# Loads, filler products and order at the two ends of a hybrid diffusion step on one core

## The chip, the cores and the metric

The kernel runs on one core of a Trainium2 chip. The metric is the device time of one execution in microseconds (us), taken as the median over runs. The profile below is that of one further execution, and its rows count from that execution's first instruction.

## What is computed

One inference step of a small backbone with two layers, in float32: layer 0 mixes tokens with a bidirectional state-space scan (SSD), layer 1 with differential attention, and each is followed by a channel mixer (up-projection, depthwise convolution, gated product, down-projection). There are 512 latent tokens and 128 context tokens, held together as 640 columns, and 1024 features, held as 8 tiles of 128 partitions. What the change touches is the very first norm with its modulation, and the very last norm:

```
m  = silu(cvec) @ mod_w + mod_b            # six rows of 1024 a layer: shift, scale, gate, twice
h  = rmsnorm(x, g) * (1 + scale) + shift   # ahead of each sub-layer
...
xs = xs + s_g2 * conv_ffn(modulate(xs, ...))
y  = rmsnorm(xs, final_norm_g)
```

`cvec` is one vector for the context tokens and another for the latent tokens.

## The kernel before

Every matrix product is made of three passes of reduced-precision products: weights and activations are split into a high and a low part (`whi`, `wlo`, `h00h`, `h00l`), and the three larger cross products are added. `cast` makes the split of one weight tile `raw`: ScalarE (ACT) copies the high part, VectorE (DVE) subtracts it for the low part. A product on plain float32 operands shows as two matmul instructions in the trace.

All instructions go through a wrapper, so almost every row of the profile has the line L95; rows are told apart by the names of their tiles. Most of the program is ordered by a planner of the framework, which walks the instructions of each engine in the order in which they were written down and lets a `high_priority` block go first. The stretch at the start, `silu_cond` and `first_tiles`, is under `manual_schedule`: each engine runs it exactly in the order written.

The start, in that order. SyncE's queue (SP) issues all loads: `c32` (the two condition vectors repeated 16 times, 128 KB), `cst` (identity, two triangles, a column block of ones and a selector, 210 KB), the eight activation tiles `x` (320 KB each), the first two weight tiles, the biases `modb` and gains, then the modulation weights `mp` in four quarters q of eight 256 KB steps k, with another weight tile behind the first quarter. The squares `sq` of x are taken by ACT for even tiles and DVE for odd ones. `rms_rows` sums them on TensorE (PE) with `ones` as weights into `ms` and runs nine small DVE instructions (`rs_v`, `rs_a`, `rs_y`) for the reciprocal root; `rms_bcast` then spreads the row over 128 partitions with four products, `nbc`. `rows(q, k0, k1)` multiplies steps k0 to k1 of quarter q of the modulation weights by the condition (`modrow`), four groups of 32 columns at a time; `finish(q)` transposes the copied row (`modt`), adds the bias (`mod`) and makes the scale `gs`. Three steps of `rows(0, ...)` stand ahead of the broadcast and five behind it. Then `bc` is copied from `nbc` by ACT, `scaled(i)` multiplies x by it on DVE, `high(i)` makes the high part of h on ACT and the full value on DVE, `low(i)` the low part on DVE, and `dense(ws, k)` does the products of feature tile k for the first weight tiles (rows `in`). The loop over q repeats this for the feature pairs 2 to 7.

The end. `project_last` computes the last three output tiles of the down-projection in two parts of the columns: part C (columns 0 to 384), then part D (384 to 640), each tile as rows `po`. `gate_add` adds a tile's result to the residual `xr` on DVE and `norm_sq` squares it on ACT. After a part a task `final_task` is queued: it sums the squares (`ms`), does the reciprocal root, broadcasts (`nbc`), and `out_tiles` multiplies the eight residual tiles (`yt`) and issues their stores. Six of part C's tiles (`CTILES`) go out as they come; the other two are held until the end of part D's reciprocal root (`self.root`). Part D's eight follow, their stores on SP and on ACT's queue in turn.

The lines around the first broadcast are

```
st = self.rms_bcast(lambda: self.wide("nbc"), sq, 0, T, D)
next(st)
self.cast(0)
self.cast(1)
rows(0, 0, 3)
```

PSUM tiles of the start come from a pool of three (`dense_ps`): one for `nbc`, two for the first two `in` tiles, and the third `in` tile takes the place of `nbc`.

Of the kernel before, what the change touches and what calls it, by code (L numbers as in the profile page):

```python
# [11 lines left out]
F32 = mybir.dt.float32  # L12
# [33 lines left out]
DOTS = 4, 24, 28, 40, 48  # L46
CTILES = 6
TH = T // 2
# [307 lines left out]
class Step:  # L356
# [129 lines left out]
    def cast(self, upto):  # L486
        while len(self.wcast) <= min(upto, len(self.units) - 1):
# [31 lines left out]
            else:  # L519
# [6 lines left out]
                else:  # L526
                    self.act(hi[:, c], r[:, c], AF.Copy)
                    self.tt(lo[:, c], r[:, c], hi[:, c].bitcast(F32), ALU.subtract)
            self.wcast[u] = (hi, lo)
# [47 lines left out]

    def rms_bcast(self, alloc, sq, t0, t1, count, wait=4, behind=False):


        n = (t1 - t0) // 4
        y = self.rms_rows(sq, t0, n, count, behind)
        yield wait
        bc = alloc()
        for j in range(4):
            self.mm(bc[:, j * n:(j + 1) * n], self.sel[:, j:j + 1].to_broadcast([P, P]), y, True, True)
        return bc

    def rms_rows(self, sq, t0, n, count, behind=False):

        ms = self.bank("m", "ms")
        gate = self.last if behind else None
        for i, s in enumerate(sq):
            for j in range(4):
                o = self.mm(ms[32 * j:32 * j + 32, :n], self.ones, s[:, t0 + j * n:t0 + (j + 1) * n],
                            i == 0, i == len(sq) - 1)
                if behind:
                    self.hold(o, [gate])
        y = self.pc.tile([P, 160], F32, tag="rs_y", name="rs_y", bufs=1)[:, :n]
        with self.urgent(1.6) if self.later else nullcontext():  # L600
# [40 lines left out]
    def norm_stats(self, half):  # L641

        tag = {"A": "y", "B": "m", "C": "y", "D": "m"}[half]
        return self.rms_bcast(lambda: self.bank(tag, "nbc"), self.nsq, *HALF[half], D, 3, half == "B")

# [54 lines left out]
    def project_last(self, h, ks, g, nextnorm, ks_last=None, parts="AB", save=False, before=(), first=None):  # L700
# [26 lines left out]
        for hf in parts:  # L727
            for grp in ((ws[0:1], ws[1:3]) if hf == "B" else (ws[0:1], ws[1:2], ws[2:3])):
                self.dense_many([(ps, w, P) for ps, w, i in grp], ks, h, hf)
                with self.tc.high_priority() if hf == "B" else nullcontext():  # L730
                    for ps, w, i in grp:
                        self.gate_add(i, ps, g, hf)
                        self.norm_sq(i, hf)
# [83 lines left out]
    def silu_cond(self, pool):  # L817

        c32 = self.slot("f", "c32", bufs=NF)[:, :KT * 32].rearrange("p (k c) -> p k c", c=32)
        self.nc.sync.dma_start(c32, self.a["c32"])  # L820
        self.s32 = pool.tile([P, KT, 32], F32, tag="s32", name="s32", bufs=1)
        self.silu_small(self.s32, c32)

    def first_tiles(self, h, pool):
# [67 lines left out]

        self.cst = self.ct([P, 3 * P + 36], "cst")
        nc.sync.dma_start(self.cst, a["cst"])
        for i in range(KT):
            xi = self.xslot(f"x{i}")
            nc.sync.dma_start(xi, a["xT"][i])
            self.x.append(xi)
        self.prefetch(1)
        self.load_consts()  # L900
        gs, sh = self.gs[0][0], self.shift(0, 0)
        load(0)
        self.prefetch(2)
        for q in range(1, 4):
# [3 lines left out]
        for i in range(KT):  # L908
            if i % 2:
                self.tt(sq[i], self.x[i], self.x[i], ALU.mult)  # L910
            else:
                self.act(sq[i], self.x[i], AF.Square)
        st = self.rms_bcast(lambda: self.wide("nbc"), sq, 0, T, D)
        next(st)
        self.cast(0)
        self.cast(1)
        rows(0, 0, 3)
        try:
            next(st)
        except StopIteration as e:  # L920
            bps = e.value
        bc = self.slot("f", "bc", bufs=NF)
        self.act(bc, bps, AF.Copy)
        scaled(0, bps)
        scaled(1, bps)
        h.extend(self.new_h("h00"))
        rows(0, 3, KT)
        finish(0)
        ws = [(self.dense_ps("in"), self.wcast[i], P if i else 64) for i in range(2)]
        half = KT // 2  # L930
        high(0)
        low(0)
        high(1)
        low(1)
        self.cast(2)
        self.wi = 3
# [1071 lines left out]
def _layout(i):  # L2008
# [5 lines left out]
    cc = np.stack([n["c_ctx"], n["c"][0]])  # L2014
    d["c32"] = np.tile(cc.reshape(2, KT, P).transpose(2, 1, 0), (1, 1, 16))
    d["cbc"] = np.broadcast_to(cc[None], (P, 2, D))
# [61 lines left out]
```

## Time and profile before

| what | value |
|---|---|
| time, median of 3 runs | 1780.58 us (1779.38 to 1784.31) |
| time of the profiled execution | 1780.09 us |
| its span, first to last instruction | 1778.3 us |
| mean granted TensorE clock | 0.996 |
| PE busy | 1744.0 us, 98% of the span |
| DVE busy | 1471.3 us, 83% |
| ACT busy | 1170.2 us, 66% |
| DMA | 300.66 MB, mean 169 GB/s |

PE is the matmul side of TensorE and PEld its weight loads; SP and ACTq rows are DMA issues. A row of the timeline gives start, duration, engine, operation with output and inputs, count of merged instructions, and in brackets the idle time of that engine before it with what ended the idle time. Durations of merged rows run from the first start to the last end.

### The profile page before, as it was taken

What the parts mean: (1) busy time and instruction counts of PE and PEld (TensorE: products, weight loads), DVE (VectorE), ACT (ScalarE), POOL (GpSimd) and SP (SyncE); (2) the same over time, 40 slices, a digit from 0 to 9 for tenths busy, and PEclk for the clock granted to TensorE, in tenths of its full rate; (3) what the DMA queues carried; (4) which work ended last, traced back from release to release, by engine and by line L of the source; (5) the groups of instructions that cost most, each with busy time, mean ns of one, the idle gap of its engine ahead of it and who ended that gap; (6) DMA issues with size and microseconds to landing.
All of it is one profiled execution on the core that took longest, in us unless ns stands there. A gap on an engine that the chain in (4) does not pass through costs nothing.

```text
span 1778.3 us, 33599 instructions
## 1 busy us (share of the span) xinstructions
PE 1744.0 (98%) x12786; PEld 1667.6 (94%) x12786; DVE 1471.3 (83%) x2947; ACT 1170.2 (66%) x2313; POOL 150.2 (8%) x180
## 2 busy tenths in 40 slices
PE   7999999999999999999999999999999999999997
PEld 5899999989989999999999999999889999999997
DVE  5789999999967879798689799899878677867686
ACT  3479696969524767666675578777547566756661
POOL 0000000000000111211210000000001012121210
PEclk9999999999999999999999999999999999999998
DMA  9744344345663686978867365666138358686882
GB/s 346 261 145 131 115 120 150 106 145 165 223 214 130 150 205 153 253 181 216 191 167 249 114 171 132 157 153 167 56 119 207 116 144 200 175 196 156 171 234 79
DMA packets 120206, 300.66 MB, mean 169 GB/s; under 512 B 13950, under 2 KB 21738, under 8 KB 120044
## 3 DMA queue, kind: packets, MB, share of 16 engines
q1 hardware_dynamic: 94636, 231.79, 39.9%
q0 software_dynamic: 24832, 66.20, 20.8%
q8 instruction: 100, 1.64, 0.4%
q14 instruction: 62, 0.51, 0.1%
q10 hardware_dynamic: 576, 0.52, 0.1%
HBM read 248.32 MB, written 34.80 MB: 159 GB/s over the span
## 4 chain that ended last, share of the span: by engine, by line
PE 72%; DVE 5%; ACT 2%; issue 1%; DMA 1%; DVEq 0%; ACTq 0%
PE up L95 27%; PE po L95 24%; PE st L95 4%; PE z L95 2%; PE q L348 2%; PE v L348 2%; PE k L348 2%; PE sl L348 2%; PE ov L348 1%; PE po L348 1%; PE yp L95 1%; PE wt L348 1%; PE nbc L95 1%; PE modrow L95 0%; DVE sm L348 0%
## 5 line engine op out<-in xcount | busy, mean ns | idle before, releaser
L95 ACT ACTIVATE whi<-raw 128x1024 fp32r<-128x1024 f32 (+2 forms) x233 | 198.8, 855 | 163.9 <-PE po L95 77.3
L95 DVE TENSOR_TENSOR wlo<-raw,whi 128x1024 fp32r<-128x1024 f32 (+2 forms) x170 | 162.4, 961 | 54.1 <-ACT whi L95 51.7
L95 PE MATMUL po<-mh,whi 128*128 128x256 f32 (+1 forms) x704 | 165.0, 307 | 0.8 <-ACT y L95 0.5
L95 PE MATMUL po<-ml,whi 128*128 128x256 f32 (+1 forms) x704 | 164.4, 306 | 0.3 <-DMA ml<-cv 0.3
L95 PE MATMUL po<-mh,wlo 128*128 128x256 f32 (+1 forms) x704 | 164.4, 306 | 0.0
L95 DVE TENSOR_TENSOR wlo<-s,whi 128x512 fp32r<-128x512 f32 x136 | 91.2, 686 | 53.4 <-ACT whi L95 53.1
L95 POOL DMA_DIRECT2D wlo<-in_w_up x62 | 54.0, 871 | 945.0 <-ACT wlo L95 646.7
L95 PEld LDWEIGHTS po<-mh,whi 128*128 128x128 f32 x704 | 126.0, 188 | 1.9 <-ACT y L95 0.9
L95 PEld LDWEIGHTS po<-ml,whi 128*128 128x128 f32 x704 | 126.2, 188 | 0.6 <-DMA ml<-cv 0.6
L95 PEld LDWEIGHTS po<-mh,wlo 128*128 128x128 f32 x704 | 126.2, 188 | 0.0
L95 PE MATMUL up<-Th,wlo 128*128 128x320 f32 x408 | 125.7, 308 | 0.0
L95 PE MATMUL up<-Tl,whi 128*128 128x320 f32 x408 | 125.3, 307 | 0.0
L95 PE MATMUL up<-Th,whi 128*128 128x320 f32 x408 | 123.7, 303 | 0.2 <-ACT uraw L95 0.2
L95 PE MATMUL up<-h11h,wlo 128*128 128x320 f32 (+2 forms) x384 | 109.0, 307 | 0.0
L95 PE MATMUL up<-h01h,wlo 128*128 128x320 f32 (+2 forms) x384 | 109.0, 307 | 0.0
L95 PE MATMUL up<-h11l,whi 128*128 128x320 f32 (+2 forms) x384 | 108.7, 307 | 0.0
L95 PE MATMUL up<-h01l,whi 128*128 128x320 f32 (+2 forms) x384 | 108.7, 307 | 0.0
L95 PE MATMUL up<-h11h,whi 128*128 128x320 f32 (+2 forms) x384 | 107.7, 304 | 0.1
L95 PE MATMUL up<-h01h,whi 128*128 128x320 f32 (+2 forms) x384 | 107.6, 304 | 0.0
L95 ACT ACTIVATE whi<-s 128x512 fp32r<-128x512 f32 x136 | 83.3, 628 | 36.9 <-DVE s L95 33.1
L95 DVE SCALAR_TENSOR_TENSOR ca<-uraw,fcw,ca 128x511 f32<-128x511 f32 (+1 forms) x176 | 86.1, 544 | 11.3 <-ACT ca L95 9.7
L95 DVE SCALAR_TENSOR_TENSOR cv<-uraw,fcw,cv 128x511 f32<-128x511 f32 (+1 forms) x176 | 85.6, 543 | 4.9 <-ACT cv L95 4.8
(574 smaller groups left out, 5415.3 us busy)
## 6 DMA issues: line engine op xcount, KB each, us to landing
raw<-in_w_up SPq DMA_DIRECT2D x88, 512.0 KB
mw<-in_modT SPq DMA_DIRECT2D x44, 512.0 KB
raw<-in_w_in SPq DMA_DIRECT2D x40, 512.0 KB
rb<-rowd SPq DMA_DIRECT2D x40, 512.0 KB
wlo<-in_w_up POOLq DMA_DIRECT2D x36, 512.0 KB, 5.8
raw<-in_w_dn SPq DMA_DIRECT2D x64, 256.0 KB
raw<-in_w_qkv SPq DMA_DIRECT2D x24, 512.0 KB
mr<-in_mod SPq DMA_DIRECT2D x44, 256.0 KB
```

The source lines that it names most:

```text
L95: return later.record(self.name, method, call, args, kw) if later else call(*args, **kw)
L348: op.real = op.call(*(x.get() if isinstance(x, Lazy) else x for x in op.args), **op.kw)
```

## The change

At the start, the condition is loaded in two columns only (8 KB) and widened on DVE after the SiLU. The constants come in three pieces: ones and selector first, the identity behind the first two weight tiles, the triangles behind the first quarter of modulation weights. The activation tiles are issued alternately on SP's and ACT's queue, ahead of all but the first constants. DVE clears a tile; TensorE runs 12 products of 128x128 by 128x512 in bfloat16 on these zeros, then one behind the sums of each of the first seven activation tiles and five behind the eighth. Five steps of modulation instead of three stand ahead of the broadcast. Behind it come the scaling of tile 0, the other three steps, `finish(0)`, and the scaling of tile 1; the scaling no longer stands behind the copy `bc`, which moves behind `high(1)`. The second half of one weight tile's low part moves behind `low(1)`.

At the end, the gate-add and the squares of part D get priority, five instead of six of part C's tiles go out before part D's root, and ten float32 products of 128x128 by 128x128 stand between part D's sums and its broadcast.

```diff
-CTILES = 6
+CTILES = 5
...
                     self.act(hi[:, c], r[:, c], AF.Copy)
-                    self.tt(lo[:, c], r[:, c], hi[:, c].bitcast(F32), ALU.subtract)
+                    minus = lambda c: self.tt(lo[:, c], r[:, c], hi[:, c].bitcast(F32), ALU.subtract)
+                    if u == 1:
+                        minus(slice(0, n // 2))
+                        self.second = lambda: minus(slice(n // 2, n))
+                    else:
+                        minus(c)
...
-        y = self.rms_rows(sq, t0, n, count, behind)
+        y = self.rms_rows(sq, t0, n, count, behind, between)
+        if fill:
+            gate, ps = self.last, self.psb.tile([P, 512], F32, tag="b", name="warm")
+            for _ in range(fill):
+                o = self.mm(ps[:, :P], self.ident, self.U, True, True)
+                self.hold(o, [gate])
         yield wait
...
+            if between:
+                between(1 if i < len(sq) - 1 else 5)
...
-        return self.rms_bcast(lambda: self.bank(tag, "nbc"), self.nsq, *HALF[half], D, 3, half == "B")
+        return self.rms_bcast(lambda: self.bank(tag, "nbc"), self.nsq, *HALF[half], D, 3, half == "B",
+                              fill=10 if half == "D" else 0)
...
-                with self.tc.high_priority() if hf == "B" else nullcontext():
+                with self.tc.high_priority() if hf in "BD" else nullcontext():
...
     def silu_cond(self, pool):
-        c32 = self.slot("f", "c32", bufs=NF)[:, :KT * 32].rearrange("p (k c) -> p k c", c=32)
-        self.nc.sync.dma_start(c32, self.a["c32"])
+        nc = self.nc
+        self.zero = self.tmp("zero").bitcast(BF16)[:, :P + 512]
+        nc.vector.memset(self.zero, 0.0)
+        self.cst = self.ct([P, 3 * P + 36], "cst")
+        nc.sync.dma_start(self.cst[:, 3 * P:], self.a["cst"][:, 3 * P:])
+        for i in range(KT):
+            xi = self.xslot(f"x{i}")
+            (nc.scalar if i % 2 else nc.sync).dma_start(xi, self.a["xT"][i])
+            self.x.append(xi)
+            if i == 1:
+                c2, s2 = (self.ct([P, KT, 2], n) for n in ("c2", "s2"))
+                nc.sync.dma_start(c2, self.a["c2"])
         self.s32 = pool.tile([P, KT, 32], F32, tag="s32", name="s32", bufs=1)
-        self.silu_small(self.s32, c32)
+        self.act(s2, c2, AF.Tanh, scale=0.5)
+        self.stt(s2, s2, 1.0, c2, ALU.add, ALU.mult)
+        nc.vector.tensor_scalar(self.s32.rearrange("p k (r c) -> p k r c", c=2),
+                                s2.unsqueeze(2).to_broadcast([P, KT, 16, 2]), 0.5, None, ALU.mult)
...
-        self.cst = self.ct([P, 3 * P + 36], "cst")
-        nc.sync.dma_start(self.cst, a["cst"])
-        for i in range(KT):
-            xi = self.xslot(f"x{i}")
-            nc.sync.dma_start(xi, a["xT"][i])
-            self.x.append(xi)
+        wps = self.dense_ps("warm")[:, :512]
+        def warm(n):
+            for _ in range(n):
+                self.mm(wps, self.zero[:, :P], self.zero[:, P:], True, True)
+        warm(12)
         self.prefetch(1)
+        nc.sync.dma_start(self.cst[:, :P], a["cst"][:, :P])
         self.load_consts()
         gs, sh = self.gs[0][0], self.shift(0, 0)
         load(0)
+        nc.sync.dma_start(self.cst[:, P:3 * P], a["cst"][:, P:3 * P])
         self.prefetch(2)
...
-        st = self.rms_bcast(lambda: self.wide("nbc"), sq, 0, T, D)
+        st = self.rms_bcast(lambda: self.wide("nbc"), sq, 0, T, D, between=warm)
         next(st)
         self.cast(0)
         self.cast(1)
-        rows(0, 0, 3)
+        rows(0, 0, 5)
...
-        bc = self.slot("f", "bc", bufs=NF)
-        self.act(bc, bps, AF.Copy)
         scaled(0, bps)
+        rows(0, 5, KT)
+        finish(0)
         scaled(1, bps)
         h.extend(self.new_h("h00"))
-        rows(0, 3, KT)
-        finish(0)
...
         high(1)
+        bc = self.slot("f", "bc", bufs=NF)
+        self.act(bc, bps, AF.Copy)
         low(1)
+        self.second()
         self.cast(2)
```

More of the change, by code (lines that the diff above doesn't have):

```diff
@@ L576, in rsqrt, with rms_bcast @@
         self.root = self.stt(y, a, 5.0, y, ALU.add, ALU.mult)
-    def rms_bcast(self, alloc, sq, t0, t1, count, wait=4, behind=False):
+    def rms_bcast(self, alloc, sq, t0, t1, count, wait=4, behind=False, fill=0, between=None):
         n = (t1 - t0) // 4
-        y = self.rms_rows(sq, t0, n, count, behind)
+        y = self.rms_rows(sq, t0, n, count, behind, between)
[4 more added lines that the diff above has]
+                self.hold(o, [gate])
         yield wait
@@ L587, in rms_bcast, with rms_rows @@
         return bc
-    def rms_rows(self, sq, t0, n, count, behind=False):
+    def rms_rows(self, sq, t0, n, count, behind=False, between=None):
         ms = self.bank("m", "ms")
@@ L2014, in _layout @@
     cc = np.stack([n["c_ctx"], n["c"][0]])
-    d["c32"] = np.tile(cc.reshape(2, KT, P).transpose(2, 1, 0), (1, 1, 16))
+    d["c2"] = cc.reshape(2, KT, P).transpose(2, 1, 0)
     d["cbc"] = np.broadcast_to(cc[None], (P, 2, D))
```

## The prediction, made before the changed kernel ran

> **What bounds the kernel now.** I read the page first. TensorE is busy nearly all the time and off the middle of the span there is little to win without fewer products.
>
> ```profile
> PE 1744.0 (98%) x12786; PEld 1667.6 (94%) x12786; DVE 1471.3 (83%) x2947; ACT 1170.2 (66%) x2313; POOL 150.2 (8%) x180
> PEclk9999999999999999999999999999999999999998
> ```
>
> The span is 1778.3 us, so PE lacks 34 us, and the change touches only the two ends. So I read the timeline of both ends, then transfers and granted clock there. The start, from the last squares to the second set of modulation rows:
>
> ```profile
> 12.15 0.82 DVE L95 TENSOR_TENSOR sq<-x 128x640 f32<-128x640 f32 x1 [0.83 <-DMA x<-in_xT]
> 13.04 0.76 PE L95 MATMUL ms<-sq,cst 128*32 128x160 f32 x8 [0.16 <-DVE sq L95]
> 13.87 0.33 DVE L95 TENSOR_SCALAR rs_v<-ms 128x160 f32<-128x160 f32 x1 [0.89 <-PE ms L95]
> 15.10 0.20 PEld L95 LDWEIGHTS modrow<-mp,s 128*32 128x32 f32 x8 [1.86 <-DMA mp<-in_modp]
> 15.79 0.20 PEld L95 LDWEIGHTS modrow<-mp,s 128*32 128x32 f32 x8 [0.48 <-DMA mp<-in_modp]
> 16.46 0.20 PEld L95 LDWEIGHTS modrow<-mp,s 128*32 128x32 f32 x8 [0.47 <-DMA mp<-in_modp]
> 17.05 2.50 PE L95 MATMUL nbc<-rs_y,cst 128*128 128x160 f32 x8
> 19.48 1.30 PE L95 MATMUL modrow<-mp,s 128*32 128x128 f32 x40
> 19.59 0.70 ACT L95 ACTIVATE bc<-nbc 128x640 f32<-128x640 f32 x1 [4.29 <-PE nbc L95]
> 20.32 1.55 DVE L95 TENSOR_TENSOR h<-x,nbc 128x640 f32<-128x640 f32 x2 [1.60 <-ACT bc L95]
> 20.85 0.28 ACT L95 ACTIVATE modrow_s<-modrow 128x128 f32<-128x128 f32 x1 [0.56 <-PE modrow L95]
> 21.79 0.16 DVE L95 TENSOR_TENSOR mod<-modt,modb 128x8 f32<-128x8 f32 x1
> 22.18 2.29 ACT L95 ACTIVATE h00h<-h,mod,gs 128x512 fp32r<-128x512 f32 x4 [1.06 <-DVE gs L95]
> 23.42 0.82 DVE L95 TENSOR_TENSOR h00l<-h,h00h 128x640 fp32r<-128x640 f32 x1 [0.43 <-ACT h00h L95]
> 24.99 1.27 PE L95 MATMUL in<-h00l,whi 128*64 128x256 f32 x4
> 26.19 1.08 PE L95 MATMUL modrow<-mp,s 128*32 128x128 f32 x32
> 27.20 0.85 PE L95 MATMUL in<-h00h,whi 128*128 128x256 f32 x4
> 28.85 1.08 PE L95 MATMUL modrow<-mp,s 128*32 128x128 f32 x32
> 31.16 0.17 DVE L95 TENSOR_TENSOR mod<-modt,modb 128x8 f32<-128x8 f32 x1 [2.67 <-PE modt L95]
> ```
>
> The last activation tile lands at 12.15, the root is ready at about 17.0, the broadcast takes 2.5, and `bc` then holds DVE until 20.32. The weights arrive 0.68 us a step (15.10, 15.79, 16.46). From 26.19 on PE goes on without a gap, so what the products of tile 0 gain stays, as long as loads keep up. The stretches and the loads of the first 30 us:
>
> ```profile
> 21.00:22.00 1.00, 0.33 (x1) 0.14 (x1) 0.96 (x4) 0.12 (x1) 0.00 (x0) 1.00 1.03 375
> 23.00:24.00 1.00, 0.95 (x3) 0.85 (x4) 0.58 (x1) 1.00 (x3) 0.00 (x0) 0.50 1.06 393
> 30.00:34.00 4.00, 4.00 (x52) 3.59 (x53) 2.34 (x7) 2.57 (x5) 0.00 (x0) 1.00 1.05 387
> DMA  0049996997999999999999999999999999999999
> GB/s 0 0 147 264 258 259 239 358 314 277 382 399 417 406 401 424 391 350 376 382 391 385 385 382 412 385 410 380 371 391 388 396 385 388 388 385 371 388 391 380
> ```
>
> In a stretch the last three columns are granted clock, transfer share and GB/s; the clock is 0.50 in 23 to 24 and 1.00 in 30 to 34, where PE is full. Transfers are saturated from 7.5 us on at about 390 GB/s, and slower before.
>
> The end:
>
> ```profile
> 1761.25 1.08 PE L95 MATMUL nbc<-rs_y,cst 128*128 128x96 f32 x8
> 1762.37 2.71 DVE L95 SCALAR_TENSOR_TENSOR yt<-xr,gains,nbc 128x384 f32<-128x384 f32 x5 [1.23 <-PE nbc L95]
> 1764.34 0.28 PE L95 MATMUL po<-ml,whi 128*128 128x256 f32 x1
> 1764.45 0.28 PE L95 MATMUL po<-mh,wlo 128*128 128x256 f32 x1
> 1766.04 0.60 DVE L95 SCALAR_TENSOR_TENSOR xr<-po,mod,xr 128x128 f32<-128x128 f32 x2
> 1766.11 0.32 PE L95 MATMUL ms<-sq,cst 128*32 128x64 f32 x8 [1.01 <-ACT sq L95]
> 1766.68 0.42 ACT L95 ACTIVATE sq<-xr 128x256 f32<-128x256 f32 x1 [0.62 <-DVE xr L95]
> 1767.15 0.44 PE L95 MATMUL ms<-sq,cst 128*32 128x64 f32 x8 [0.72 <-ACT sq L95]
> 1767.66 0.22 DVE L95 TENSOR_SCALAR rs_v<-ms 128x64 f32<-128x64 f32 x1 [1.01 <-PE ms L95]
> 1769.96 1.14 DVE L95 SCALAR_TENSOR_TENSOR yt<-xr,gains,nbc 128x384 f32<-128x384 f32 x2
> 1770.07 1.94 PE L95 MATMUL nbc<-rs_y,cst 128*128 128x64 f32 x8 [2.48 <-DVE rs_y L95]
> 1772.05 3.22 DVE L95 SCALAR_TENSOR_TENSOR yt<-xr,gains,nbc 128x256 f32<-128x256 f32 x8 [0.95 <-PE nbc L95]
> 1767.00:1770.00 3.00, 0.44 (x8) 0.20 (x8) 2.03 (x10) 0.10 (x1) 0.00 (x0) 0.51 0.17 65
> ```
>
> The last product ends at about 1764.7, but its gate-add waits behind scaled tiles until 1766.04, and the last broadcast takes 1.94 for 64 columns at half clock, against 1.08 for 96 columns before.
>
> **Start: loads.** Ahead of the modulation weights 338 KB (c32 128, cst 210) become 90 (18 + 8 + 64), so 248 KB less, 0.65 us at 390 GB/s. Behind the first quarter the triangles give back 128 KB, so later quarters gain 0.3. The small pieces: three transfers more; their rows are at least free and at most as dear as the 128-packet transfer of 210 KB that they replace (0.5); I take free. The second queue: transfers are 9 tenths busy in the slow stretch too, so I price it at 0, up to 2.0 (rival two).
>
> So step k4 of quarter 0, before 15.10 + 4 x 0.68 = 17.8, lands at 17.2; k7, before 19.9, at 19.2. The last x lands at about 11.4 (0.65 to 0.8 earlier).
>
> **Start: zeros.** PE can start after DVE's clear, at about 1.2 us (0.1 to 0.8 for the clear, by the smallest and the 128x640 DVE rows). No 512-column bfloat16 product stands in the trace; products of 256 columns start 0.11 to 0.12 apart (1764.34, 1764.45), and 512 columns are an estimate of 0.23, or 0.47 at half clock. Twelve take 2.8 to 5.6 us and are over before the first sums (6 us). With the clock up, sums of a tile (0.76 cold, by the granted clock about 0.5 warm) and one filler are 0.7, under the 0.83 between tiles, so they cost nothing. Five behind the last take 1.2, inside the root's 3.2.
>
> **Start: broadcast.** Root: last x 11.4 + 0.82 + 0.1 + 0.5 + 3.2 gives 16.0. But now five steps stand ahead on PE, and k4 lands at 17.2; so the broadcast begins at 17.5, 0.45 later than before. On a warm clock it takes 1.3 instead of 2.5: the same eight instructions in the attention layer, at full clock, are
>
> ```profile
> 1294.25 1.29 PE L348 MATMUL obc<-rs_y,cst 128*128 128x160 f32 x8
> ```
>
> It ends at 18.8 (before 19.55). The other three steps end with k7 at 19.5 (before 20.8), since 0.26 a step hides under the 0.68 of loading. From there to `h00h` it took 1.4; 0.3 of that was DVE busy on the second scaling, which now stands behind `gs`; 1.1 remain, so `h00h` starts at 20.6, 1.6 earlier. DVE then does the second scaling (0.75), the full value (0.75) and `h00l` (0.82): `h00l` ends 2.35 after `h00h` starts, before 2.06. So it ends at 22.95 instead of 24.24, and tile 0's last four products, 0.74 warm instead of 1.27, end at 23.8 instead of 26.2. The copy `bc` (0.70) moves on ACT behind four activations (2.29) and ends about 23.6, ahead of its reader and of the third `in` tile. DVE's later pile (half a low part 0.6, a full one 1.2, two scalings 1.55) ends at 27.9, before 28.5, and DVE then stood idle 2.67 ahead of the next `mod` (31.16): no cost.
>
> Do loads follow? Quarter 1's steps: after 19.9 come 512 KB (1.3) and 0.68 a step, k3 at 23.9 and k7 at 26.6; with 0.3 less 23.6 and 26.3. The two sets of rows would start at 23.8 and 26.5 (before 26.19 and 28.85). They fit by 0.2, and each later set has more slack. **Start: 2.3 us**, with ends 0.3 (below) and 4.
>
> **End.** With priority the gate-adds of the second and third D tile go ahead of scaled tiles that are ready. The last product at 1764.7, at worst one scaled tile of 0.54 (2.71 for five) in flight, so the gate-add ends at 1765.5 instead of 1766.6; square, sums, root follow: the root 1.1 earlier, at 1768.8 (bounds 0.5 and 1.3, for none to two scaled tiles ahead). The fifth scaled tile fits into the 1.0 that DVE waits there. One more held tile costs DVE 0.54 behind the root: three end at 1770.5 instead of 1771.1. The ten products are twenty instructions; eight of 96 columns took 0.11 each, those of 160 columns 0.14, so 0.12, 2.4 us, beside a root of 2.3: at most 0.3 late. The broadcast then begins at 1769.1 and, warm, takes 0.9, over before DVE is free at 1770.5. The eight tiles, 3.22, thus begin at 1770.5 instead of 1772.05. Their stores (1 MB) keep pace as before; three C stores go out 0.6 earlier than two did. **End: 1.5 us** (bounds -0.8 and 1.8).
>
> **Sum.** 2.3 + 1.5 = 3.8 off the profiled execution's 1780.09 (span 1778.3 and 1.8 around it): 1776.3. That execution stood 0.5 under the median of the three runs, so the median to compare is 1776.8. The planner between the ends may set a few instructions otherwise; no row prices that, and the three runs' own distance (1.2 below and 3.7 above the median) bounds it.
>
> **Rivals.**
> One: the clock falls while PE waits for k0 to k4 (0.27 of work in each 0.68), so the broadcast takes 2.5. Then it ends at 20.0, three steps end at 20.75, `h00h` starts at 21.85, and tile 0 is done at 25.1: 1.1 instead of 2.3, so 1778.0. For it: at 1767 the clock fell to 0.51 although PE had idled only 1.01 and 0.72 us; at 23 it fell after 1.6 us of work in 3.4. Against: the five fillers and the broadcast close the gap from both sides. The Trainium skill ("TensorE: Matmul & The Clock Gate", Part 1: The HAM clock gate) has the clock fall after an idle window of about 3.4 us, so never here, and would give 1776.8; the trace disagrees, the clock was 0.51 with no such gap, so the rival keeps its chance.
>
> Two: the slow loads of 1.5 to 7.5 us (mean 265 GB/s) were the single queue's and the wide-row constants' doing. At 395 the missing 0.78 MB are 2.0 us, and since steps k4, k7 and quarter 1 all wait for loads, all of it counts: 1774.8. Against: the engines were mostly 9 tenths busy then. The Trainium skill ("DMA: Bandwidth & Descriptors", Issuing engines are not separate DMA queues) says that issuing from several engines saves no more than issue time, which speaks against this rival: by it 1776.8, by the slow stretch 1774.8. No run here has yet issued loads from two queues.
>
> Three: the end's filler runs at half clock. Twenty at 0.24 are 4.8 us from 1766.5, so the broadcast starts near 1770.9 and the last tiles gain nothing or lose up to 0.8: 1778.3 to 1779.1. For it: the fall at 1767 above. Against: the root comes 1.1 earlier and the fillers follow the sums at once.
>
> Four, the slower side: zeros do not raise the clock. Then a tile's sums and filler cost 0.76 + 0.47 = 1.23 on PE, over the 0.83 between loads, and PE becomes the start's bound: from 6.9 eight tiles end at 16.7, fillers at 19.0, five steps at 21.5, the broadcast at 24.0, and `h00h` starts at 25.9, 3.7 late. Less 1.5 at the end: 1782.8. It decides as soon as sums and filler exceed 0.83. Against: the broadcast itself raised the clock within one stretch.
>
> **How the numbers follow.** Main case 0.5 (1775.0 to 1778.3), rival one 0.2, two 0.15, three 0.1, four 0.05. The prediction is the main case, 1776.8. For 8 in 10 I go down past rival two by the runs' own 1.2 (1773.4) and up past rivals one and three together (1779.5) by as much (1780.8). A measurement can tell 0.3%, 5.3 us, so 1775.2 and below is faster: four fifths of rival two and three tenths of the main case, 0.27. Slower, above 1785.9, needs rival four and a reordered middle: 0.02. The rest, 0.71, is the same.
>
> **What would show it.** Start: `ms` of 160 columns at 0.5 per eight; five `modrow` sets then `nbc` at 17.5 for 1.3; `h00h` at 20.6; the second quarter's first rows at 23.8. End: gate-adds within 0.5 of the last `po`, `rs_v` at 1766.5 less the start's gain, `nbc` under 1.0, and a gap from root to the first 256-column `yt` of 1.7. Wrong would be: x landing no earlier, `nbc` at 2.5, a clock under 1.00 behind 1766, or waits for `mp` in the later quarters.

## The result, and the profile after

The changed kernel takes 1785.41 us (median of 22 runs, 1781.37 to 1788.17), the kernel before 1780.82 on the same chip (22 runs, 1778.35 to 1784.93): ratio 1.0024, 95% interval 1.0018 to 1.0030. The forecast was 1776.8 with a range up to 1780.8; the change is 0.24% slower instead of 0.2% faster. The profiled execution of the changed kernel took 1781.37 us, the lowest of its runs (span 1779.4, before 1778.3). So the traces explain about 1 us directly, and the median has to be settled by the experiments.

The timeline of the changed kernel, beginning (columns: start, length, engine, line, operation, tiles; in brackets the idle time before and what ended it):

```profile
0.74 5.26 ACTq L95 DMA_DIRECT2D x<-in_xT  x4
1.26 5.30 PE L95 MATMUL warm<-zero 128*128 128x512 bf16 x12 [1.26 <-DVE zero L95]
6.03 1.28 ACT L95 ACT_TABLE_LOAD   x1 [6.03 <-DMA x<-in_xT]
7.45 0.72 ACT L95 ACTIVATE sq<-x 128x640 f32<-128x640 f32 x1
9.71 0.93 SPq L95 DMA_DIRECT2D mp<-in_modp  x2
12.35 0.80 SPq L95 DMA_DIRECT2D mp<-in_modp  x2
12.36 0.83 DVE L95 TENSOR_TENSOR sq<-x 128x640 f32<-128x640 f32 x1 [2.08 <-DMA x<-in_xT]
13.33 0.48 PE L95 MATMUL ms<-sq,cst 128*32 128x160 f32 x8
16.99 0.43 PE L95 MATMUL modrow<-mp,s 128*32 128x128 f32 x8 [0.96 <-DMA mp<-in_modp]
18.29 0.43 PE L95 MATMUL modrow<-mp,s 128*32 128x128 f32 x8 [0.88 <-DMA mp<-in_modp]
18.65 1.35 PE L95 MATMUL nbc<-rs_y,cst 128*128 128x160 f32 x8
19.93 0.86 PE L95 MATMUL modrow<-mp,s 128*32 128x128 f32 x24
21.96 1.20 ACT L95 ACTIVATE h00h<-h,mod,gs 128x512 fp32r<-128x512 f32 x2 [0.82 <-DVE gs L95]
25.61 1.94 PE L95 MATMUL modrow<-mp,s 128*32 128x128 f32 x32
```

Read it from the bottom: tile 0 starts (`h00h`) at 21.96 because the first quarter's products end at 20.79 (before: 20.78, so up to here nothing is gained), because step k4 came only at 18.29. Between two steps lie 1.3 us there instead of 0.68. Higher up is the cause: SP issues two `mp` steps at 9.71, then nothing until 12.35. At 12.36 the square of the last x tile starts, so SP waited for that tile's landing (its third step waits for the semaphore that the last x load raises). ACT shows the same at 6.03: its table load waits for an x load, and the first square comes at 7.45.

The same stretches as sums (columns: stretch, its length, PE busy with the count of its instructions, granted clock, share of transfers, GB/s), changed kernel; before had 389 and 387 GB/s here:

```profile
7.00:13.50 6.50, 5.28 (x68) 1.00 1.02 367
13.50:19.50 6.00, 4.14 (x59) 1.00 0.92 285
```

What SP's DMA queue waited for in the first 20 us (total, times, longest), changed kernel:

```profile
SPq L95 <- DMA x<-in_xT: 4.0, 3, 2.0
```

Before, the same waits came in small pieces:

```profile
SPq L95 <- DMA x<-in_xT: 3.6, 7, 0.8
```

Clock at the start of the changed kernel, cut along its clock changes:

```profile
17.29:20.70 3.41, 2.53 (x47) 1.00 0.99 336
20.70:24.10 3.40, 1.70 (x11) 1.00 1.03 384
24.10:27.51 3.41, 3.32 (x38) 0.50 1.06 393
```

The zeros did raise the clock, and the broadcast took 1.35. But after a stretch in which PE was busy for 1.70 of 3.40 us (it waits for `h00h`) the next 3.41 us ran at half clock, just where tile 0's products and the second quarter's rows stand (1.94 for 32).

The end of the changed kernel:

```profile
1767.39 0.28 PE L95 MATMUL po<-mh,wlo 128*128 128x256 f32 x1
1767.70 0.61 DVE L95 SCALAR_TENSOR_TENSOR xr<-po,mod,xr 128x128 f32<-128x128 f32 x2
1768.82 0.32 PE L95 MATMUL ms<-sq,cst 128*32 128x64 f32 x8 [0.68 <-ACT sq L95]
1769.07 2.50 PE L95 MATMUL warm<-cst 128*128 128x128 f32 x20
1769.28 0.22 DVE L95 TENSOR_SCALAR rs_v<-ms 128x64 f32<-128x64 f32 x1
1771.58 4.80 DVE L95 SCALAR_TENSOR_TENSOR yt<-xr,gains,nbc 128x384 f32<-128x384 f32 x11
1771.69 1.07 PE L95 MATMUL nbc<-rs_y,cst 128*128 128x64 f32 x8
```

From the last `po` to the root's first instruction are 1.9 us (before 3.2), and the broadcast takes 1.07 instead of 1.94, beside scaled tiles on DVE. But all of it stands later: the last `po` came at 1764.45 before.

Where it slipped shows in one row a kernel, the feed-forward products of `Th` and `whi` (ns min/median/max, first and last start). Before:

```profile
L95 PE MATMUL up<-Th,whi x408: 302/303/418, 657.6 to 1716.3; 128*128 128x320 f32 x136
```

Changed kernel:

```profile
L95 PE MATMUL up<-Th,whi x408: 304/309/417, 657.7 to 1719.2; 128*128 128x320 f32 x136
```

The first such product is 0.1 late, the last 2.9. The products stand in two stretches, one in each layer; the time between the stretches is no longer than before (490.1 us before, 489.7 in the changed kernel). In the last 220 us PE is full in both kernels, and yet they hold fewer products in the changed one. First before, then changed:

```profile
1500.00:1720.00 220.00, 219.88 (x1526) 1.00 0.76 176
```

```profile
1500.00:1720.00 220.00, 220.00 (x1519) 1.00 0.76 174
```

Seven products of about 0.145 us are the 1 us that this stretch loses. The modelled length of one went from 303 to 309, the mean distance from its start to the next from 140 to 147 ns, and 408 x 7 ns is 2.9 us. The only thing that the change did to these products is their place in memory: `c2` and `s2`, 64 bytes a partition each, lie in the pool of constants, and everything allocated behind it on that side (weights, activations) moves by 128 bytes, while `Th`, `Tl` and the residual on the other side stay.

In the profiled execution the bill is 0.1 at 657, 2.8 more by 1716, and 1.8 back at the end (from the first product of part D, 1756.24 before and 1759.14 after, to the end of the span): 1.1, as the spans say.

### The profile page after: what moved, and what is told of

It reads as the page before. It is cut to its first block, busy times and chain, and to the rows that moved or that the text cites. A ratio compares the mean times of both kernels' runs of the same rounds, so it can differ in the third digit from the quotient of the medians.

```text
span 1779.4 us, 33690 instructions
## 1 busy us (share of the span) xinstructions
PE 1753.6 (99%) x12830; PEld 1674.1 (94%) x12830; DVE 1471.8 (83%) x2949; ACT 1170.8 (66%) x2313; POOL 150.2 (8%) x180
## 4 chain that ended last, share of the span: by engine, by line
PE 90%; DVE 5%; DMA 3%; ACT 1%; issue 1%; SPq 0%; DVEq 0%; ACTq 0%
PE up L95 28%; PE po L95 24%; PE z L95 5%; PE x L95 5%; PE st L95 5%; PE bc L95 3%; PE yp L95 3%; PE v L348 2%; PE q L348 2%; PE k L348 2%; PE sl L348 2%; PE ov L348 2%; PE po L348 1%; DMA mp<-in_modp 1%; PE wt L348 1%; DMA raw<-in_w_in 1%
## 5 line engine op out<-in xcount | busy, mean ns | idle before, releaser
L95 DVE TENSOR_TENSOR wlo<-raw,whi 128x512 fp32r<-128x512 f32 (+3 forms) x171 | 163.0, 960 | 54.0 <-ACT whi L95 53.6
```

The lines of the kernel that those rows point to most:

```text
L95: return later.record(self.name, method, call, args, kw) if later else call(*args, **kw)
```

## The experiments

All times are medians in us; "before" is the kernel before, run on the same chip beside each group. Ratios are to it, with 95% intervals; they are taken from the single runs and are not quotients of the medians (e4 stands at 1.0012 by the medians). The groups e1 to e8, e9 to e12 and e13 to e16 ran on three chips, so across groups the ratios are the ones to compare.

| kernel | time | before | ratio | span of its profile |
|---|---|---|---|---|
| e1 before, shifted 128 bytes | 1784.46 | 1780.85 | 1.0016 (1.0007 to 1.0025) | 1781.8 |
| e2 change without the shift | 1781.63 | 1780.85 | 1.0000 (0.9991 to 1.0009) | 1778.0 |
| e3 end alone | 1779.43 | 1780.85 | 0.9986 (0.9977 to 0.9995) | 1777.2 |
| e4 start alone, no shift | 1783.04 | 1780.85 | 1.0005 (0.9994 to 1.0015) | 1777.6 |
| e5 e4 on one queue | 1782.13 | 1780.49 | 1.0012 (1.0003 to 1.0020) | 1780.7 |
| e6 e2 on one queue | 1782.31 | 1780.49 | 1.0012 (1.0001 to 1.0022) | 1780.8 |
| e7 e5 without zeros | 1781.08 | 1780.49 | 1.0001 (0.9993 to 1.0010) | 1781.4 |
| e8 before, shifted 64 bytes | 1781.61 | 1780.49 | 1.0006 (0.9997 to 1.0014) | 1779.8 |
| e9 e5, small loads on POOL | 1780.55 | 1780.26 | 1.0002 (0.9994 to 1.0011) | 1786.3 |
| e10 e6, gap filled | 1781.18 | 1780.26 | 1.0002 (0.9993 to 1.0011) | 1779.7 |
| e11 e6, small loads on POOL and gap filled | 1777.76 | 1780.26 | 0.9985 (0.9977 to 0.9994) | 1775.8 |
| e12 e3, gap filled | 1777.78 | 1780.26 | 0.9986 (0.9978 to 0.9995) | 1776.8 |
| e13 e11, gap not filled | 1779.72 | 1779.63 | 1.0000 (0.9991 to 1.0009) | 1775.5 |
| e14 e11 on two queues | 1776.89 | 1779.63 | 0.9986 (0.9977 to 0.9995) | 1774.4 |
| e15 e11 with the shift | 1782.26 | 1779.63 | 1.0014 (1.0004 to 1.0023) | 1778.1 |
| e16 e11, three steps ahead | 1779.13 | 1779.63 | 0.9995 (0.9986 to 1.0004) | 1775.1 |

### The shift by itself: e1, e2, e8

e1 takes the kernel before and adds 128 unused bytes; e2 takes the change and puts the two tiles elsewhere; e8 is e1 with 64 bytes (`[P, 16]`).

```diff
 # e1
         self.cst = self.ct([P, 3 * P + 36], "cst")
+        self.pc.tile([P, 32], F32, tag="padc", name="padc", bufs=1)
 # e2
-                c2, s2 = (self.ct([P, KT, 2], n) for n in ("c2", "s2"))
+                c2, s2 = (self.slot("f", n, bufs=NF)[:, :2 * KT].rearrange("p (k c) -> p k c", c=2) for n in ("c2", "s2"))
```

> The kernel before with one unused tile of 128 bytes a partition in the pool of constants, which moves every left-hand buffer behind it by 128 bytes, as the two small condition tiles of the change do, and nothing else. Theory A (address shift: products whose weights are in shifted buffers and whose activations are not, up<-Th,whi, take 147 ns apart instead of 140): the feed-forward stretches run some 1.3 us longer each, the D part of the end starts 2.5 to 3 us later, and the time is 1783.4 (+2.6). Theory B (the middle drifts by another cause, such as the order of instructions or chance between executions): no change, 1780.8, and up<-Th,whi stays at 140 ns.

> The changed kernel with its two small condition tiles in the rotating buffers instead of the pool of constants, so that the later buffers keep the addresses of before modulo 512 bytes. Theory A: the drift of 2.6 us in the middle goes, the time falls to about 1782.8 (from 1785.4), and 2 us above before remain for the start. Theory B: it stays at 1785.4.

> The kernel before with an unused 64 bytes a partition in the constants pool instead of 128: weights and activations of the left-hand pools move by 64 bytes, the sums Th and Tl stay. In before, the weights whi stand 128 bytes from Th modulo 256; a shift of 128 gave both the same place modulo 256. If the cost is that coincidence, a shift of 64 leaves the products of Th and whi at 140 ns and the time within 1 of before. If any distance but before's costs, the spacing is about 147 ns and the time 3 above, as with 128. Moving operands that no longer start on a multiple of 64 bytes don't arise, since 64 is kept.

The same row of e1, of e2 and of e8:

```profile
L95 PE MATMUL up<-Th,whi x408: 304/309/418, 657.0 to 1719.8; 128*128 128x320 f32 x136
```

```profile
L95 PE MATMUL up<-Th,whi x408: 302/303/415, 658.9 to 1717.9; 128*128 128x320 f32 x136
```

```profile
L95 PE MATMUL up<-Th,whi x408: 304/307/417, 657.9 to 1718.0; 128*128 128x320 f32 x136
```

Against before (657.6 and 1716.3) e1 goes from 0.6 early to 3.5 late with not one instruction changed, e2 from 1.3 late to 1.6 late, e8 from 0.3 to 1.7. So a shift of 128 bytes costs 3 to 4 us over the two stretches, 2.9 of them in these 408 products, and taking it away gives that back. The second stretch alone, in which PE is full, parts all the profiles: from its first to its last such product it takes 283.5 or 283.6 us in the fourteen kernels without a shift, 285.0 to 285.2 in the three with 128 bytes (changed kernel, e1, e15), and 284.5 in e8. By time it is +3.6 in e1 and -3.8 from the changed kernel to e2 (medians; the changed kernel ran in another group). With 64 bytes the products stand between (307; 145 ns from start to start), the drift is 1.4, and the time, +1.1, isn't told from none. The guess of a coincidence modulo 256 bytes alone falls, and so does the guess that any other distance costs the same. Distance between the two operands isn't the whole of it either: the products of `h01h` and `whi`, both of which move by the same 128 bytes, also grow, from a mean of 303 to 305. What about the addresses counts stays open.

### The two ends apart: e3, e4

e3 is the kernel before with the changed end (`CTILES = 5`, the ten products, priority for D); e4 is e2 with the end of before.

> The kernel before with the changes of the end alone (priority of part D, five tiles out first, ten products as filler). Theory A: from the first product of part D to the end 20.3 us instead of 22.1, as in the profile of the change, and the time 1779.0 (-1.8). Rival: the filler is caught at half clock in most executions, since the window of the clock is free-running, and the gain is 0 to 0.5: 1780.5.

> The changed kernel with the end of before, and with the two small tiles in the rotating buffers (no shift). Theory A (the start is not faster, since later loads became slower and the last activation tile waits): the start is 0 to 2 us later than before, 1781 to 1783. Rival (the start gains in most executions, and the profile was an exception): 1779 or less.

The end is worth 0.14% by the ratio (2.5 us), 1.4 us by the medians and 1.7 in the profile (20.4 us from the first product of part D to the end, before 22.1); its root and broadcast have the lengths of the changed kernel's. The timeline of e3:

```profile
1769.22 4.80 DVE L95 SCALAR_TENSOR_TENSOR yt<-xr,gains,nbc 128x384 f32<-128x384 f32 x11
1769.33 1.07 PE L95 MATMUL nbc<-rs_y,cst 128*128 128x64 f32 x8
```

The start alone gains nothing: 2.2 above before by the medians, ratio 1.0005. Its trace repeats the gap in the loads (the stretch 13.5 to 19.5 of e4):

```profile
13.50:19.50 6.00, 4.14 (x58) 1.00 0.95 302
```

Medians add up: 3.6 (shift) - 1.4 (end) + 2.2 (start) = 4.4, against 4.6 measured. The ratios are less kind: 0.16 - 0.14 + 0.05 = 0.07%, each with some 0.09 either way, so about 0.16 for the sum, against 0.24 (0.18 to 0.30). They meet only at the edge.

### What the loads wait for: e5, e6, e9

e5 is e4 with all x tiles on SP, e6 the same with the changed end, e9 is e5 with the four small loads on POOL.

```diff
 # e5, e6
-            (nc.scalar if i % 2 else nc.sync).dma_start(xi, self.a["xT"][i])
+            nc.sync.dma_start(xi, self.a["xT"][i])
 # e9: c2, cst[:, :P], modb and gains
-        nc.sync.dma_start(self.cst[:, :P], a["cst"][:, :P])
+        nc.gpsimd.dma_start(self.cst[:, :P], a["cst"][:, :P])
...
```

> The new start without the shift of addresses and with the end of before, and all eight x tiles loaded by SP instead of alternately by SP and ACT. Theory (loads take eight completion semaphores in turn, so the second queue only makes ACT and then SP wait in order for an older load): ACT's table load and first square come some 1.5 to 2 us earlier, SP issues the steps of the modulation without a gap of 2 us, the transfer rate in 13 to 19 us is back near 390 GB/s, steps k3 and k4 land 0.7 apart, and the broadcast of 160 columns begins by 17.6 and takes 1.3; time 1.0 to 2.0 below the kernel with two queues and 0.5 to 2 below before. Rival (the rate falls because of the additional small pieces, whatever the queue): the rate stays near 300 GB/s in 13 to 19 us, k4 lands at 18.0 or later, time as with two queues.

> The same with the reordered end: the whole change without the shift of addresses and with one queue. If start, end and middle add up, 1.4 below the kernel of one queue with the end of before, so 1777 to 1778.5 where before has 1780.8. If the end's gain hangs on the state in which the middle arrives, the difference is under 0.7.

> The new start on one queue, without the shift of addresses and with the end of before, but the four small loads (c2, the transposing third of the constants, modb, gains) issued by POOL instead of SP. Theory (each load on SP waits for the landing of the load eight places back; the small pieces use up places, so step k0 is issued only when x5 has landed, x4 before the change): SP goes on from the weights of the first projection straight to the steps, k0 is issued by about 8.0 instead of 9.3 to 10.3, the rate stays near 390 GB/s, k4 lands by 17.2 and the broadcast begins by 17.5. Rival (the rate of the memory alone sets it, 0.65 less data but as many small transfers): k4 lands at 17.7 or later and issue times don't matter. Time: between none and 1 below the same start with the pieces on SP, since the clock may still fall behind the broadcast.

My theory fell in e5: with one queue the long wait of SP was gone and the first square early, and yet k4 came no sooner. The timeline of e5:

```profile
7.87 0.33 SPq L95 DMA_DIRECT2D cst<-in_cst  x1
8.66 0.33 SPq L95 DMA_DIRECT2D modb<-in_modb  x1
9.47 0.33 SPq L95 DMA_DIRECT2D gains<-in_gains  x1
10.31 5.42 SPq L95 DMA_DIRECT2D mp<-in_modp  x8
17.13 0.42 PE L95 MATMUL modrow<-mp,s 128*32 128x128 f32 x8 [0.23 <-DMA mp<-in_modp]
18.25 0.43 PE L95 MATMUL modrow<-mp,s 128*32 128x128 f32 x8 [0.69 <-DMA mp<-in_modp]
```

SP issues `cst`, `modb`, `gains` and k0 0.8 apart, the pace at which x tiles land. In the built program the loads of SP and ACT take eight completion semaphores in turn, so a load is issued only when the load eight places earlier has landed. Each of the three small loads uses a place and waits as long as a large one; the change added one such place ahead of k0, which in e5 waits for x5 where it had waited for x4 before. And with small loads in three of the eight places, fewer bytes are under way. e9 tests it; timeline of e9:

```profile
7.99 6.54 SPq L95 DMA_DIRECT2D mp<-in_modp  x8
17.61 0.43 PE L95 MATMUL modrow<-mp,s 128*32 128x128 f32 x8 [0.24 <-DMA mp<-in_modp]
17.96 2.45 PE L95 MATMUL nbc<-rs_y,cst 128*128 128x160 f32 x8
```

k0 is issued at 7.99, the steps come 0.67 apart, the rate in 13.5 to 19.5 is 390 GB/s (e5 342), and k4 is there at 17.6. Over all the profiles the rate parts cleanly: 285 to 372 GB/s in the seven kernels of the new start with small loads on SP, 383 to 391 in the six with them on POOL. The start of k4's products does not: 17.2 to 18.3 in the seven, 16.7 to 17.6 in e9, e11, e13 and e14, but 18.9 in e15. So the issue times and the rate are shown to follow the small loads, and an earlier k4 only in part.

By time e9 is at 1.0002 and e5 at 1.0012, which does not part them. And that execution of e9 had a broadcast of 2.45: the clock had fallen at 18.1, and again at 24.9, 100.0 and 1339.0, and it took 1788.06, 7.5 above its kernel's median. e6 took 2.15 for the broadcast and its clock fell at 18.1, 24.9 and 100.0; the end reordered gave nothing there (1.0012 for e5 and e6), against the 1.4 expected.

### What the clock follows: e7, e10, e12

e7 is e5 without the products on zeros; e10 is e6 with six more behind `finish(0)`; e12 is e3 with five products of constants at the same place.

```diff
 # e10
         rows(0, 5, KT)
         finish(0)
+        warm(6)
 # e12
         rows(0, 3, KT)
         finish(0)
+        ps = self.dense_ps("warm")
+        for _ in range(5):
+            self.mm(ps[:, :P], self.ident, self.U, True, True)
```

> As the kernel of one queue with the end of before, but without the 24 products on zeros. If the zeros raise the clock: sums of a tile take 0.76 instead of 0.48, the broadcast of 160 columns takes 2.3 to 2.6 instead of 1.3, and the start is 0.8 to 1.5 later. If the five steps of the modulation ahead of the broadcast would raise the clock by themselves, the broadcast takes 1.3 here too and the time is the same within 0.5.

> The whole change without the shift of addresses and on one queue, with six more products on zeros behind the turn of the first quarter's modulation, where PE stood idle 1.3 waiting for h00h. Theory (the clock is judged in windows of 3.41 us whose position is free; a window with PE half busy or less is followed by one at half clock, and the window around 20 to 24 was that in nearly every kernel): PE is 0.7 or more busy there, the clock does not fall between 20 and 29, tile 0's products take 2.2 in all instead of 3.0 and the second quarter's eight half rows 1.1 instead of 1.9; time 1 to 1.5 below the same kernel without them. Rival (the fall comes from something else, such as the mean since the start): the fall at 23 to 28 stays and the time with it.

> The kernel before with the reordered end alone, and five products of constants in the gap behind the turn of the first quarter's modulation (its start is else that of before: no products on zeros, loads as before). If the fall of the clock at 22 to 28 comes from the half-filled window, it stays away here, or comes in fewer executions, and the time is 0.7 to 1.5 below the kernel with the reordered end alone. If the clock is not yet up at that point whenever the windows lie badly, the fillers run at half clock, end late by up to 1, and the time is the same within 0.7.

Without the zeros the broadcast takes 2.31 and the sums 0.76, so the zeros do what they are for; but e7 is no slower than e5 (1.0001 and 1.0012), so a warm clock up to 24 was worth nothing that could be measured. In all the profiles the clock changes on a grid of 3.41 us whose place differs from execution to execution (the first rise stood at 4.2 to 7.2 with zeros, at 19.4 to 21.9 without). The fall between 22.8 and 25.3 is in eleven of the twelve profiles without fillers in the gap, and in none of the six with them. The exception, e2, had the gap split between two windows. e10's clock fell at 18.5 instead, after a window with PE 0.48 busy. By time e10 (1.0002 against 1.0012 for e6) and e12 (0.9986, as e3) don't show the fillers' worth by themselves.

### Both repairs, and one taken away at a time: e11, e13 to e16

e11 is e6 with the edits of e9 and e10. The others undo one thing each: e13 the fillers in the gap, e14 the single queue, e15 the place of `c2` and `s2`, e16 the five steps (three again).

> The whole change without the shift of addresses and on one queue, with both edits: small loads issued by POOL, and six more products on zeros in the gap. If both theories hold: broadcast by 17.5, no fall at 20 to 29, second quarter's first rows at 23.8 to 24.3, and a time of 1776 to 1778, the least of all. If the start's gain is used up by waits for the modulation's loads in the quarters behind, 1778 to 1780.

> The repaired kernel (no shift, one queue, small loads on POOL, gap filled, end reordered), with the six products on zeros in the gap taken out again. If the half-filled window costs: a fall of the clock at 18 to 28 in the profile and a time 1 to 1.5 above the repaired kernel's 1777.8. If the fall costs nothing because loads or ACT bound the quarters behind, the time stays within 0.5.

> The repaired kernel with the x tiles loaded by SP and ACT in turn again. Theory (the second queue puts ACT's table load and squares behind its fourth load, which waits for x0's landing, and lets the shared semaphores couple the two queues): first square at 7.0 or later instead of about 5.4, the sums later, and SP's steps wait for x7's place; broadcast 0.3 to 1 later, time 0.3 to 1 above 1777.8. Rival (the second queue is free once the small pieces are away): within 0.3.

> The repaired kernel with c2 and s2 in the pool of constants again, so that weights and activations stand 128 bytes on. If the shift's cost is a matter of the products' spacing alone it adds as before: 3 to 3.8 above 1777.8, products of Th and whi 309 ns median instead of 303, and 7 or 8 fewer products in 220 us of the second layer's feed-forward. If it cost only together with the late start, it is below 1.5.

> The repaired kernel with three steps of the modulation ahead of the broadcast instead of five, as before the change. The broadcast then waits for the root only: k2 lands at about 16.2, so it begins at 16.3 to 16.9 instead of 17.9, but the remaining five steps end with the load of k7 as before, and h00h waits for them: same time within 0.5. If the order of five steps costs by itself (the first scaling on DVE comes later and pushes the next ones), the time is 0.5 to 1 lower.

Timeline of e11:

```profile
17.88 1.35 PE L95 MATMUL nbc<-rs_y,cst 128*128 128x160 f32 x8
22.05 1.12 PE L95 MATMUL in<-h00h,whi 128*128 128x256 f32 x4
24.31 1.08 PE L95 MATMUL modrow<-mp,s 128*32 128x128 f32 x32
```

and its clock, with the gap filled:

```profile
18.14:21.56 3.42, 2.97 (x37) 1.00 1.03 389
21.56:24.97 3.41, 3.29 (x37) 1.00 1.05 386
```

In this trace the start gains most of what was forecast. The second quarter's rows begin at 24.31 (said 23.8, before 26.19) and the feed-forward products come 2.3 early (655.3 to 1714.3, before 657.6 to 1716.3). Its time is 0.15% below before (0.06 to 0.23). That this start is faster by time is not shown, though: e12, which has the old start with its gap filled and the same end, has the same median on the same chip (1777.78 and 1777.76). In the profile of e11 the lead is 2.0 at the first product of part D, but from there to the end it took 21.6 us (before 22.1, changed kernel 20.3), with a broadcast as early behind the last `po` as in the others and later stores.

e10 is e11 with the small loads back on SP: 1.0002 against 0.9985, 3.4 us by the medians on the same chip, with intervals that barely overlap (0.9993 and 0.9994). In its profile k4's products start at 18.18, and the clock falls at 18.5 after a window in which PE waited for them, so that the broadcast takes 2.50.

e13: the fall is back (23.5), the second quarter's rows take 1.94, and the third quarter's begin at 28.40 instead of 26.95, 1.45 later. By time it is 1.0000 against 0.9985, 2.7 us, with intervals that just overlap (0.9991 and 0.9994). The granted clock of all executions agrees: 0.998 or 0.999 in the 12 of e11, 0.995 to 0.998 in the 11 of e13.

e14: the second queue costs nothing once the small loads are away. It was expected later by 0.3 to 1; instead the last steps and the broadcast come 0.8 earlier. Timeline of e14:

```profile
8.24 4.93 SPq L95 DMA_DIRECT2D mp<-in_modp  x8
17.08 1.35 PE L95 MATMUL nbc<-rs_y,cst 128*128 128x160 f32 x8
23.74 1.08 PE L95 MATMUL modrow<-mp,s 128*32 128x128 f32 x32
```

SP still waits for x loads there (5.3 us in three waits), but at k0, with large loads under way, and the rate is 383 GB/s in 13.5 to 19.5. At 1776.89 this is the lowest median of all, though by the ratio it is level with e11, and it is the change as made, but for three edits: `c2` and `s2` out of the pool of constants, small loads on POOL, the gap filled.

e15: the shift lengthens the products as before. The row of e15, where e11 had 303 and 655.3 to 1714.3:

```profile
L95 PE MATMUL up<-Th,whi x408: 304/309/415, 656.5 to 1718.2; 128*128 128x320 f32 x136
```

From 1.1 ahead of before to 1.9 behind it: 3.0. By time it is 1.0014 against 0.9985, about 5 us, more than the 3 to 3.8 expected. Its profile shows a late start too, which the shift does not explain:

```profile
18.94 0.43 PE L95 MATMUL modrow<-mp,s 128*32 128x128 f32 x8 [1.78 <-DMA mp<-in_modp]
```

This is k4, issued at 11.20 as in e11 (11.31), at a rate of 390 GB/s. So a step can land late with the small loads on POOL as well; why is open.

e16: the broadcast begins at 15.94 instead of 17.88 and the second quarter's rows at 24.31, to the hundredth as in e11. Five steps or three ahead of it make no difference in the trace, since `h00h` waits for k7 either way; the times (0.9995 and 0.9985) don't part them.

## Why the prediction was wrong

In the profiles the sum came out so: the start 0.1 us behind where 2.3 ahead was said, the middle 2.8 behind where nothing was said, the end 1.8 ahead where 1.5 was said. That is 1.1 slower instead of 3.8 faster, and the medians are 4.6 apart.

**The middle, taken at nothing: the largest failure.** The prediction put it as "The planner between the ends may set a few instructions otherwise; no row prices that". The instructions hardly moved; the addresses did. It measured 2.8 in the trace of the changed kernel, 3 to 4 in e1 and e15. The words "248 KB less" counted the new tiles as bytes to load and never as room in memory that moves what lies behind it.

**Start, loads: failed.** "the small pieces ... I take free" and the order of issue failed. The last x tile was to land at 11.4 and landed at about 12.4 (before 12.15), which is one of the signs that the prediction named; k4 was to land at 17.2 and its products started at 18.29. "Three transfers more" is a miscount, there are two, one of them ahead of k0. What was counted were bytes; what also counts is which load a new one has to wait for. With the small loads off that queue k4's products start at 16.7 to 17.6 in e9, e11, e13 and e14, around the 17.2 that was said, but at 18.9 in e15; and with them on it 17.2 to 17.4 occurs too (e2, e6, e7). So the waits and the lower rate are shown, but not that they are the whole delay.

**Start, second queue priced at 0: right by time,** rival two's 2.0 did not come. In the change itself the fourth load on ACT held ACT's table load and squares back (first square 7.45 instead of 5.24). The Trainium skill ("DMA: Bandwidth & Descriptors", Issuing engines are not separate DMA queues) has a second issuing engine save issue time alone; e14 against e11 (0.9986 and 0.9985) agrees.

**Start, zeros and broadcast: right in size.** Sums 0.48 (said 0.5), broadcast 1.35 (1.3), five fillers inside the root. But e7, which leaves the zeros out, was no slower than e5. Rivals one and four did not come in the changed kernel's profile; e6, e9 and e10 show that rival one's fall does come when the window lies badly (2.15 to 2.50 for the broadcast).

**Start, tile 0: failed by the clock.** From the end of the first quarter's products to `h00h` it took 1.2 (said 1.1). The estimate took tile 0's last products at full clock, though, and the clock fell at 24.1, as it had fallen at 22.8 before. The prediction quoted the fall at 23 ("after 1.6 us of work in 3.4") and used it for rival one only, not on the gap of 1.3 us ahead of `in`, which its own steps kept. Second quarter's rows: said 23.8, measured 25.61; 1.36 of the 1.8 is the late `h00h`, most of the rest the half clock.

**End: right in the trace.** Said 1.5, measured 1.8 in the profile and 1.4 by the medians of e3. On the new start it is not seen by time: e2 against e4 is 0.05% lower, e6 against e5 the same, each with an interval of about 0.1% either way. Gate-adds follow the last `po` at once, the ten products take 2.50 (2.4), the broadcast 1.07 (0.9), and the clock stays at 1.00 until 1775. Rival three did not come.

**What stays open.** The median of the changed kernel is 4.0 above its profiled execution; half-clock windows may explain a part. Of its 22 executions the two with a granted clock of 0.998 (the profiled one is one of them) took 1782.2 us on average, the 17 with 0.996 or 0.997 took 1785.2, the two with 0.994 took 1787.9. One window of 3.41 us at half clock lowers the mean clock by 0.001 and cost 1.45 us in e13, so one or two more of them would be 1.5 to 2.9 of the 3.0 us between the first two groups. But the executions at 0.996 and at 0.997 do not differ (1785.0 and 1785.3), and only one execution of the changed kernel has a profile, so this stays open. How an address comes to lengthen a product is not explained.

## What to carry to other kernels

A tile put into a pool moves everything behind it: compare addresses, not only instructions, and where a full engine slows without a wait, look at the length of one product in one row before and after. Count loads by places as well as by bytes: where loads share a few completion semaphores, a small load ahead of large ones costs as long a wait as a large one, and is worth trying on another engine's queue. A filler in the half-empty window ahead of work that matters kept the clock up there in all six profiles that have one; warming earlier stretches that wait for loads gained nothing that could be measured. And where a gain of 2 us shows in the trace, look whether the runs show it as well.

## What the runs showed of the hardware

Moving weights and activations by 128 bytes, while `Th` stayed, made the 320-column products of `Th` and `whi` start 147 instead of 140 ns apart, 64 bytes 145, with the same instructions (means of 408; e1, e8).

The clock is judged in windows of 3.41 us on a grid that does not start with the program. The Trainium skill ("TensorE: Matmul & The Clock Gate", Part 1: The HAM clock gate) says so too, and has it fall after an idle window. Here a half-idle one was enough, in the start, near 100 us and near 1335 us. The stretches of e9 around 100 us:

```profile
96.67:100.08 3.41, 1.51 (x11) 0.98 0.74 271
100.08:103.49 3.41, 3.41 (x16) 0.52 0.46 160
```

PE was busy 1.51 of 3.41 us (0.44) and the next window ran at half clock; the falls ahead of the end in these profiles followed shares of 0.35 to 0.67, all but two of them 0.54 or less. The share isn't all of it, as far as the modelled ends of products let it be read. In the window that begins between 1327 and 1336 us, shares of 0.45 or 0.46 were followed by a fall in four profiles (e5, e7, e9, e12), while six with shares of 0.46 to 0.51 passed without one (before, changed kernel, e1, e3, e4, e8), and so did a window of 0.45 in e14 (from 4.2 us). What else decides is open. Products on zeros count as work: in e14 they start 0.43 us apart at first and 0.22 from 4.2 us on, where the granted clock rises, with nothing else on PE until then.
